# Shared PSUM banks and alternating row halves in the preparation of an RWKV-7 recurrence, inside a two-layer diffusion backbone

## The chip, the cores and the metric

The kernel runs on one core of a Trainium2 chip. The metric is the device time of one execution in microseconds (us). A core has a matrix engine (TensorE, PE in the profile, with its weight loads as PEld), a vector engine (VectorE, DVE), a scalar engine (ScalarE, ACT), a general one (GpSimd, POOL) and a sync engine (SyncE, SP), which here issues the DMAs. Matrix products land in PSUM, which this kernel uses as eight banks of 128 rows by 512 fp32 numbers.

## What is computed

The reference is a flow-matching backbone on 256 context tokens and 512 latent ones (768 together), model width 1024, all fp32. Layer 0 mixes tokens with latent attention (MLA, 8 heads) beside eight RWKV-7 heads of 64; layer 1 with state-space heads beside windowed attention. Each layer ends in a feed-forward part. The change lies in the RWKV-7 part of layer 0, which computes, per head and in both directions,

```python
def rwkv_scan(r, w, k, v, kk, a, state0, reverse):
    def step(s, inp):
        r_t, w_t, k_t, v_t, kk_t, a_t = inp
        sa = jnp.einsum('bhij,bhj->bhi', s, -kk_t)
        s = s * w_t[:, :, None, :] + sa[..., None] * (kk_t * a_t)[:, :, None, :] + v_t[..., None] * k_t[:, :, None, :]
        return s, jnp.einsum('bhij,bhj->bhi', s, r_t)
    ...
    s_final, ys = lax.scan(step, state0, xs, reverse=reverse)
```

The kernel does this in 12 chunks of 64 tokens. Within a chunk the step's dependence on earlier tokens is a triangular system, so each chunk needs the inverse of a 64x64 triangular matrix before the recurrence over chunks can use it.

## The kernel before

The program is written in Python as one long sequence. A scheduler then fixes each engine's order of instructions from that sequence and from its own simulation of the times; each engine runs its instructions in that fixed order and waits at each for its inputs and for a free buffer. Buffers come from named pools: a pool hands out its buffers in turn, and the next user of a buffer waits until the last reader of the one before is done. So both the order and the waits follow from the sequence and from the sizes of the pools. All products that a helper issues carry its line, L267; tiles tell them apart.

PSUM in the stretch concerned: `acc`, two tiles of two banks each, for the projections; `bkp`, one bank, for the layers' modulation (`ada_group`) and small products; `gk`, two banks; `iv`, one bank; and `px1` and `px0`, one bank each for the two halves of the recurrence. `px1` and `px0` are opened when `gk`, `iv`, `bkp` and `accp` are closed in the program, and take over banks of these. After that come `accm` (four banks) and `mb` (two).

The eight heads are four pairs p; the two heads of a pair lie in rows 0 to 63 and 64 to 127 (`par` 0 and 1). For each pair the program does three things:

- `features(p)` (L596): projections, then per direction d the tiles `ar` (two factors of a product, made by three POOL operations of 768 columns at L674, L673, L676), `EC` (small POOL copies at L669 to L672) and `bk` (brought into place by DMA; tile `bkt`). A POOL operation at L649 makes the bonus term.
- `rwkv_prep(p)` (L699): for each direction and each of three groups of four chunks, two sets of four products `bk` by `ar`, one for each row half, 64 rows deep and 128 columns wide, each set in a `gk` bank of its own. ScalarE copies the diagonal blocks out of the bank to `LS` (L721, twice a set) and one to `PB` (L722), VectorE masks the rest (L723, L726), DMAs bring it to the recurrence's records. Then four transposes into another `gk` bank (L732) and a ScalarE copy of it (L733). `LS` has one buffer; POOL's MEMSET at L701 is its first writer.
- `rwkv_inverse(p)` (L738): a VectorE transpose of `LS` to `I`, then 60 POOL operations (L748 a product into a temporary `w`, L750 its sum into `I`, each waiting for the one before), a select (L751) and a MEMSET (L753), which invert the 32x32 diagonal blocks of all the pair's chunks by substitution. VectorE transposes the result to `PN` and `TT` (L755 to L758). Then the joins to 64x64 blocks, for each direction: 24 products `PN` by `PB` into an `iv` bank, a copy to `w1` (L767), 24 products `TT` by `w1` into an `iv` bank, a copy back (L773), a DMA to the records (L775). The temporary `w` and `w1` share two buffers.

The program's order is preparation 0, preparation 1, inverse 0, preparation 2, inverse 1, preparation 3, inverse 2, inverse 3. Then comes `rwkv_chain`, 12 steps times two halves (half 0 has the pairs 0 and 1, half 1 the pairs 2 and 3); each half-step writes two `b` tiles in its `px` bank. Beside it the program writes latent attention: sums of squares, key products (`acc`), value products (`mb`, 36 of them), query products (`acc`), eight heads of attention (`ax` and others), and then the output projection of both mixers.

Of the kernel before, what the change touches and what calls it, by code (L numbers as in the profile page):

```python
# [17 lines left out]
P = 128  # L18
# [192 lines left out]
def hybrid_kernel(ctx: ExitStack, tc: tile.TileContext, a, out):  # L211
# [4 lines left out]
    def open_pool(name, side=None, psum=False):  # L216
        kw = dict(side=side, space=PSUM) if psum else dict(side=side)
        PL[name] = tc.alloc_tile_pool(name=name, bufs=1, reuse_waits="tile", **kw)

    def close_pool(*names):  # L220
        for n in names:
            PL.pop(n).release()

    def T(pool, shape, tag, bufs=1, dt=F32):
        uid[0] += 1
        return PL[pool].tile(shape, dt, tag=tag, bufs=bufs, name=f"{tag}_{uid[0]}")
# [4 lines left out]
    def F(dt=F32):  # L231
        return row_tile("sb", "f", NF, dt)
# [12 lines left out]
    def bank():  # L245
        return T(bankp[0], [P, 512], bankp[1], bankp[2])
# [14 lines left out]
    def mm(o, lhsT, rhs, start, stop, shared=False):  # L261
        i = -1
        if pace["pins"] is not None:
            pace["t"] += o.free_size() / 2400 * (4 if rhs.dtype == F32 else 1) * (0.5 if o.shape[0] == 64 else 1)
            i = min(pace["base"] + int(pace["t"] / pace["per"]), len(pace["pins"]) - 1)
        with tc.issue_after(pace["pins"][i]) if i >= 0 else nullcontext():
            ins = nc.tensor.matmul(o, lhsT=lhsT, rhs=rhs, start=start, stop=stop, skip_group_check=shared)  # L267
        pe_last[0] = ins.ins
# [7 lines left out]
    open_acc("accp", 2)  # L276
    open_bank("bkp", 1)
    open_pool("gk", psum=True)
    open_pool("iv", psum=True)
    con = T("sb", [P, NCO], "con")  # L280
    pv = T("sb", [P, NPV], "pv")
    ones = T("sb", [P, P], "ones")
# [247 lines left out]
    H = (slice(0, 64), slice(64, P))  # L530
# [49 lines left out]
    GC = 4  # L580
# [111 lines left out]
        return ars, bks  # L692

    def gbank():
        return T("gk", [P, 512], "gk", 2)

    Q = [(slice(64 * q, 64 * q + 32), slice(64 * q + 32, 64 * q + 64)) for q in range(2)]

    def rwkv_prep(p, ars, bks):  # L699
        LS = T("pp", [P, 32, 32], "LS", 1)  # L700
        nc.gpsimd.memset(LS[:, :, 24:32], 0.0)  # L701
        PB = T("pp", [P, 2 * NCH, 32], "PB", 2)
        for d in range(2):
            bk, ar = bks[d], ars[d]
            for gi in range(NG):
                i0 = d * NCH + gi * GC
                cg = slice(gi * GC, gi * GC + GC)
                s0 = (gi * GC + 4 * d) % NCH
                rec = REC[p // 2][:, s0:s0 + GC, d, p % 2]
                tg = T("pp", [P, GC, 192], "tg", 2)  # L710
                w = T("pp", [P, GC, 2, CH], "W", 2)
                for par in range(2):
                    hb, hk = H[par], H[1 - par]
                    r0 = Q[par][0]
                    b = gbank().rearrange("p (c x) -> p c x", x=P)
                    for c in range(GC):
                        mm(b[:, c], lhsT=bk[hb, gi * GC + c].rearrange("p a t -> p (a t)"),
                           rhs=ar[hb, gi * GC + c].rearrange("p a t -> p (a t)"), start=True, stop=True)
                    for q in range(2):
                        rr = Q[par][q]  # L720
                        nc.scalar.copy(LS[rr, :, i0:i0 + GC].rearrange("p t i -> p i t"), b[rr, :, 32 * q:32 * q + 32])  # L721
                    nc.scalar.copy(PB[r0, i0:i0 + GC], b[r0, :, 32:64])  # L722
                    tt(out=w[hk], in0=b[hk].rearrange("p c (a t) -> p c a t", a=2),  # L723
                       in1=mk[hk].rearrange("p (a t) -> p a t", a=2).unsqueeze(1).to_broadcast([64, GC, 2, CH]),
                       op=ALU.mult)
                    tt(out=tg[hb, :, 128:192], in0=b[hb, :, 64:128],  # L726
                       in1=mk[hb, 64:].unsqueeze(1).to_broadcast([64, GC, CH]), op=ALU.mult)
                    dma(rec[hk, :, 128 * par:128 * par + 128], w[hk].rearrange("p c a t -> p c (a t)"))

                b = gbank()  # L730
                for c in range(GC):
                    nc.tensor.transpose(b[:, c * P:(c + 1) * P], bk[:, gi * GC + c].rearrange("p a t -> p (a t)"), ident)  # L732
                nc.scalar.copy(tg[:, :, 0:128], b.rearrange("p (c x) -> p c x", x=P))  # L733
                dma(rec[:, :, 256:448], tg)

        return LS, PB

    def rwkv_inverse(p, LS, PB):  # L738

        I = T("pp", [P, 32, 32], "I", 2)  # L740
        TT = T("pp", [P, 32, 64], "TT", 1)
        nc.vector.transpose(I.rearrange("p t s -> p (t s)"), LS.rearrange("p t s -> p (t s)"))
        Jf = T("pp", [P, 384], "w1", 2)
        eng = nc.gpsimd if INV_POOL[p] else nc.vector
        for m in range(1, 31):
            n = 31 - m
            tmp = Jf[:, :n * m].rearrange("p (t s) -> p t s", s=m)
            eng.tensor_tensor(out=tmp, in0=I[:, m + 1:, m:m + 1].to_broadcast([P, n, m]),  # L748
                              in1=I[:, m:m + 1, :m].to_broadcast([P, n, m]), op=ALU.mult)
            eng.tensor_tensor(out=I[:, m + 1:, :m], in0=I[:, m + 1:, :m], in1=tmp, op=ALU.add)  # L750
        nc.gpsimd.affine_select(out=I, in_=I, pattern=[[1, 32], [-1, 32]], compare_op=ALU.is_gt, fill=0.0,  # L751
                                base=0, channel_multiplier=0)
        nc.gpsimd.memset(I.rearrange("p t s -> p (t s)")[:, 0:1024:33], 1.0)  # L753
        PN = T("pp", [P, 32, 32], "PN", 1)
        nc.vector.transpose(PN, I.rearrange("p t s -> p s t"))  # L755
        for r0, r1 in Q:
            nc.vector.transpose(TT[r0, :, :32].rearrange("p i t -> p t i"), I[r0])
            nc.vector.transpose(TT[r1, :, 32:].rearrange("p i t -> p t i"), I[r1])  # L758
            nc.gpsimd.memset(TT[r1, :, :32], 0.0)
        for d in range(2):  # L760
            b = T("iv", [P, 512], "iv", 1)[:, :384].rearrange("p (c x) -> p c x", x=32)
            w1 = T("pp", [P, 384], "w1", 2).rearrange("p (c x) -> p c x", x=32)
            for c in range(NCH):
                for r0, r1 in Q:
                    mm(b[r1, c], lhsT=PB[r0, d * NCH + c], rhs=PN[r0, :, d * NCH + c], start=True, stop=True)
            for r0, r1 in Q:
                nc.scalar.copy(w1[r1], b[r1])  # L767
            b2 = T("iv", [P, 512], "iv", 1)[:, :384].rearrange("p (c x) -> p c x", x=32)
            for c in range(NCH):
                for r0, r1 in Q:  # L770
                    mm(b2[r0, c], lhsT=w1[r1, c], rhs=TT[r1, d * NCH + c, 32:], start=True, stop=True)
            for r0, r1 in Q:
                nc.scalar.copy(TT[r0, d * NCH:d * NCH + NCH, 32:], b2[r0])  # L773
            for cs_, st_ in CMAP[d]:
                dma(REC[p // 2][:, st_, d, p % 2, 448:512], TT[:, d * NCH + cs_.start:d * NCH + cs_.stop])  # L775
# [3 lines left out]
    for p in range(4):  # L779
        fe = features(p)  # L780
        cur = rwkv_prep(p, *fe)
        if pend:
            rwkv_inverse(p - 1, *pend)
        pend = cur
        ada_group(0, p + 2, mods0, "pj", NAW)
    rwkv_inverse(3, *pend)
    close_pool("pp", "pa", "pj", "iv", "gk", "bkp")


    open_pool("rw0", "left")  # L790
# [164 lines left out]
    for tb in range(6):  # L955
        b = bank()
        n = 0
        for k in range(2):
            for (xt, wt) in ((kvh, wvh), (kvl, wvh), (kvh, wvl)):
                mm(b, lhsT=xt[k][:, tb * P:(tb + 1) * P], rhs=wt[:, 4 * k:4 * k + 4].rearrange("p a b -> p (a b)"),  # L960
                   start=n == 0, stop=n == 5)
# [248 lines left out]
    def sdbank():  # L1210
        return T("sd", [P, 512], "sd", 3)
# [77 lines left out]
    for g in range(2):  # L1289
# [7 lines left out]
        t = T("sx", [P, 6, P], "btm", 2)  # L1297
# [11 lines left out]
    for g in range(2):  # L1309
# [10 lines left out]
        for d in range(2):  # L1320
            hprev = None
            hs = slice(32 * d + 8 * g, 32 * d + 8 * g + 8)
            for i, c in enumerate(seq[d][:-1]):
# [4 lines left out]
                b = sdbank()  # L1328
# [9 lines left out]
        b = sdbank()  # L1338
# [8 lines left out]
        for c in range(2, 6):  # L1347
# [20 lines left out]
            b = sdbank()  # L1368
# [41 lines left out]
    t = F()  # L1410
# [136 lines left out]
    for g in range(2):  # L1547
# [12 lines left out]
        b = bank()  # L1560
# [70 lines left out]
```

## Time and profile before

| | |
|---|---|
| median of three timed runs | 2265.78 us (2265.28 to 2267.42) |
| the profiled execution's own time | 2264.21 us |
| its span in the profile | 2262.3 us |
| mean clock granted to TensorE | 0.956 of full speed |
| busy: PE, PEld | 2076.5 us (92%), 1640.9 us (73%) |
| busy: DVE, ACT, POOL | 1346.3 us (60%), 928.3 us (41%), 506.2 us (22%) |

Times in the profile count from the span's start. In a row of the timeline stand the start, the busy time, the engine, the line in the kernel, the operation, what it writes and reads, rows and columns, and the count of instructions that the row sums up; in brackets how long the engine stood idle just before it and what ended that. In a row of the windows view stand the stretch's bounds, its length, then for PE, PEld, DVE, ACT and POOL the busy time with the number of instructions, then the granted clock, the mean busy share of the DMA engines and GB/s. In a row of the grouped view the three numbers are the shortest, the middle and the longest duration in ns, then the first start and the last.

### The profile page before, as it was taken

The numbers are of one execution on the slowest core, as the hardware profiler recorded it, in microseconds if no ns is written. First come the engines' busy times: TensorE is split into PE (matmuls) and PEld (weight loads), VectorE is DVE, ScalarE is ACT, GpSimd is POOL, SyncE is SP. The second block draws the span as 40 slices with busy tenths as digits, with TensorE's granted clock in tenths as the row PEclk, the third lists the DMA queues.
The fourth block names the chain that finished last, engine by engine and source line by source line (L and its number), as shares of the span: only waits on it lengthen the run. The fifth ranks groups of instructions, "written<-read, shape, count | busy, mean of one in ns | idle before, by whom it ended". The sixth has DMA issues, their size and how long they took to land.

```text
span 2262.3 us, 33884 instructions
## 1 busy us (share of the span) xinstructions
PE 2076.5 (92%) x13558; PEld 1640.9 (73%) x13558; DVE 1346.3 (60%) x2081; ACT 928.3 (41%) x1434; POOL 506.2 (22%) x486
## 2 busy tenths in 40 slices
PE   5888889788998999999999998898888999999997
PEld 3666667566654878888888886786565667888886
DVE  5566965666766465445354444678985556554555
ACT  4445663532355244233132335544344345342434
POOL 0027686611223010000000004442641230000000
PEclk9999999698999999999999999999889999999998
DMA  8477777669741441211212213213426032323231
GB/s 303 125 206 206 182 211 195 211 190 320 259 165 42 154 139 62 61 66 57 75 53 60 75 58 114 96 52 117 133 71 172 28 111 79 96 92 98 84 116 61
DMA packets 181069, 282.58 MB, mean 125 GB/s; under 512 B 63328, under 2 KB 118656, under 8 KB 177840
## 3 DMA queue, kind: packets, MB, share of 16 engines
q1 hardware_dynamic: 180912, 280.42, 40.6%
q8 instruction: 107, 1.75, 0.3%
q14 instruction: 50, 0.41, 0.1%
HBM read 225.43 MB, written 47.33 MB: 121 GB/s over the span
## 4 chain that ended last, share of the span: by engine, by line
PE 65%; DVE 6%; ACT 5%; DMA 5%; issue 3%; POOL 1%; SPq 0%; DVEq 0%; ACTq 0%; POOLq 0%
PE acc L267 49%; PE sd L267 3%; PE o L267 3%; PE wo L267 2%; PE ab L267 2%; PE b L267 2%; DMA u<-sp_v 1%; DVE E L1359 1%; DMA aw<-ada 1%; POOL I L750 1%; PE ax L267 1%; PE ad L267 1%; POOL w L748 1%; DMA E<-sp_ac 1%; ACT L416 1%
## 5 line engine op out<-in xcount | busy, mean ns | idle before, releaser
L267 PE MATMUL acc<-s,whi 128*128 128x512 f32 (+1 forms) x3104 | 759.8, 356 | 3.0 <-ACT s L463 3.0
L267 PEld LDWEIGHTS acc<-s,whi 128*128 128x128 f32 x3104 | 546.0, 188 | 97.3 <-ACT s L463 4.8
L267 PE MATMUL acc<-s,wlo 128*128 128x512 f32 (+1 forms) x1552 | 462.0, 358 | 0.0
L267 PE MATMUL acc<-h,whi 128*128 128x256 f32 (+2 forms) x1248 | 321.1, 371 | 15.9 <-ACT p L639 5.0
L325 ACT CAST whi<-wraw 128x1024 fp32r<-128x1024 f32 (+5 forms) x228 | 210.0, 923 | 282.3 <-PE acc L267 218.0
L267 PEld LDWEIGHTS acc<-s,wlo 128*128 128x128 f32 x1552 | 289.5, 188 | 42.9 <-DVE wlo L326 0.7
L267 PEld LDWEIGHTS acc<-h,whi 128*128 128x128 f32 (+1 forms) x1248 | 223.7, 197 | 68.4 <-issue 15.4
L326 DVE TENSOR_TENSOR wlo<-wraw,whi 128x1024 fp32r<-128x1024 f32 (+5 forms) x205 | 218.7, 1069 | 44.2 <-ACT whi L325 43.6
L381 DVE SCALAR_TENSOR_TENSOR s<-acc,pv,s 128x511 f32<-128x511 f32 (+1 forms) x132 | 87.0, 659 | 246.2 <-ACT s L380 245.4
L380 ACT ACTIVATE s<-acc,pv 128x512 f32<-128x512 f32 (+1 forms) x132 | 93.4, 708 | 235.4 <-PE acc L267 224.2
L484 DVE SCALAR_TENSOR_TENSOR x<-acc,mods,x 128x512 f32<-128x512 f32 (+1 forms) x136 | 79.4, 620 | 175.0 <-PE acc L267 174.8
L267 PE MATMUL acc<-h,wlo 128*128 128x256 f32 (+2 forms) x624 | 179.5, 362 | 0.0
L434 POOL TENSOR_TENSOR f<-f,f 128x768 f32<-128x768 f32 (+1 forms) x24 | 31.3, 1306 | 635.0 <-ACT f L429 625.1
L267 PEld LDWEIGHTS acc<-h,wlo 128*128 128x128 f32 (+1 forms) x624 | 119.3, 195 | 21.9 <-issue 5.6
L1178 POOL TENSOR_TENSOR s<-w,s 128x256 f32<-128x256 f32 x6 | 5.0, 855 | 381.3 <-ACT s L416 381.3
L383 DVE SCALAR_TENSOR_TENSOR s<-acc,pv,s 128x511 f32<-128x511 f32 (+1 forms) x132 | 87.2, 660 | 4.2
L750 POOL TENSOR_TENSOR I<-I,w 128x30 f32<-128x30 f32 (+14 forms) x120 | 76.7, 639 | 9.0
L748 POOL TENSOR_TENSOR w<-I 128x30 f32<-128x30 f32 (+14 forms) x120 | 69.4, 578 | 34.6 <-PE iv L267 25.8
L387 ACT CAST s<-s 128x768 fp32r<-128x768 f32 (+1 forms) x44 | 32.0, 727 | 106.1 <-DVE s L1151 106.1
L326 POOL TENSOR_TENSOR wlo<-wraw,whi 128x1024 fp32r<-128x1024 f32 x23 | 61.7, 2686 | 59.6 <-ACT whi L325 56.1
L1359 DVE TENSOR_SCALAR E<-E,acm 128x128 f32<-128x128 f32 x128 | 61.2, 546 | 14.6 <-ACT G L1356 14.6
L723 DVE TENSOR_TENSOR W<-gk,con 64x512 f32<-64x512 f32 x48 | 32.8, 683 | 51.2 <-ACT PB L722 47.3
(390 smaller groups left out, 3347.3 us busy)
## 6 DMA issues: line engine op xcount, KB each, us to landing
aw<-ada SPq DMA_DIRECT2D x96, 512.0 KB, 5.8
wraw<-up SPq DMA_DIRECT2D x88, 512.0 KB, 3.5
rec<-sp_rec SPq DMA_DIRECT2D x24, 1024.0 KB, 9.7
wraw<-w_in SPq DMA_DIRECT2D x47, 512.0 KB, 3.8
wraw<-down SPq DMA_DIRECT2D x40, 384.0 KB, 3.1
sp_rec<-tg SPq DMA_DIRECT2D x24, 384.0 KB, 3.3
E<-sp_ac SPq DMA_DIRECT2D x16, 512.0 KB, 5.5
x<-xT SPq DMA_DIRECT2D x16, 384.0 KB, 5.9
```

Source lines behind the costliest of these rows:

```text
L267: ins = nc.tensor.matmul(o, lhsT=lhsT, rhs=rhs, start=start, stop=stop, skip_group_check=shared)
L325: nc.scalar.copy(hi[:, :kt], raw[:, :kt])
L326: (eng or tt)(out=lo[:, :kt], in0=raw[:, :kt], in1=hi[:, :kt].bitcast(F32), op=ALU.subtract)
L380: act(o[rows, t0:t0 + n], ps[rows, po:po + n], AF.Identity, scale=w1, bias=b)
L381: stt(out=o[rows, t0 + 1:t0 + n], in0=ps[rows, po:po + n - 1], scalar=w0, in1=o[rows, t0 + 1:t0 + n], op0=ALU.mult, op1=ALU.add)
L383: stt(out=o[rows, t0:t0 + n - 1], in0=ps[rows, po + 1:po + n], scalar=w2, in1=o[rows, t0:t0 + n - 1], op0=ALU.mult, op1=ALU.add)
L387: nc.scalar.copy(hi, src)
L484: stt(out=x[:, t0:t0 + n], in0=ps[:, po:po + n], scalar=mods[:, c6 * 8 + m, c:c + 1], in1=x[:, t0:t0 + n], op0=ALU.mult, op1=ALU.add)
L723: tt(out=w[hk], in0=b[hk].rearrange("p c (a t) -> p c a t", a=2), in1=mk[hk].rearrange("p (a t) -> p a t", a=2).unsqueeze(1).to_broadcast( ...
L748: eng.tensor_tensor(out=tmp, in0=I[:, m + 1:, m:m + 1].to_broadcast([P, n, m]), in1=I[:, m:m + 1, :m].to_broadcast([P, n, m]), op=ALU.mult)
L750: eng.tensor_tensor(out=I[:, m + 1:, :m], in0=I[:, m + 1:, :m], in1=tmp, op=ALU.add)
L1359: ts(out=e[:, h], in0=e[:, h], scalar1=acm[:, c, h0 + h:h0 + h + 1], scalar2=0.0, op0=ALU.subtract, op1=ALU.min)
```

## The change

The pool `iv` is gone, and `gk` has three banks in place of two. The products, the transposes and the joins of the inverse all take their bank from `gk` in turn. In a preparation's group, both product banks are taken first, and the eight products are written alternately for the two row halves; what follows each half is unchanged.

```diff
     open_pool("gk", psum=True)
-    open_pool("iv", psum=True)
...
     def gbank():
-        return T("gk", [P, 512], "gk", 2)
+        return T("gk", [P, 512], "gk", 3)
...
+                gb = [gbank().rearrange("p (c x) -> p c x", x=P) for _ in range(2)]
+                for c in range(GC):
+                    for par in range(2):
+                        mm(gb[par][:, c], lhsT=bk[H[par], gi * GC + c].rearrange("p a t -> p (a t)"),
+                           rhs=ar[H[par], gi * GC + c].rearrange("p a t -> p (a t)"), start=True, stop=True)
                 for par in range(2):
                     hb, hk = H[par], H[1 - par]
                     r0 = Q[par][0]
-                    b = gbank().rearrange("p (c x) -> p c x", x=P)
-                    for c in range(GC):
-                        mm(b[:, c], lhsT=bk[hb, gi * GC + c].rearrange("p a t -> p (a t)"),
-                           rhs=ar[hb, gi * GC + c].rearrange("p a t -> p (a t)"), start=True, stop=True)
+                    b = gb[par]
...
         for d in range(2):
-            b = T("iv", [P, 512], "iv", 1)[:, :384].rearrange("p (c x) -> p c x", x=32)
+            b = gbank()[:, :384].rearrange("p (c x) -> p c x", x=32)
...
-            b2 = T("iv", [P, 512], "iv", 1)[:, :384].rearrange("p (c x) -> p c x", x=32)
+            b2 = gbank()[:, :384].rearrange("p (c x) -> p c x", x=32)
...
-    close_pool("pp", "pa", "pj", "iv", "gk", "bkp")
+    close_pool("pp", "pa", "pj", "gk", "bkp")
```

The scheduler answers with another order on every engine between the first product of preparation 0 and the output projection. In the rows below, the line numbers of the changed kernel are one or two off those of the kernel before, and the numbers behind the tiles' names tell buffers apart; they differ between the kernels for the same tile.

The first place is TensorE in the first group of preparation 3: `gk` is written by the products (`ar`, `bkt`) of the two row halves and by the transposes (`con`). Before, in the same group:

```order
L267 MATMUL acc_3771<-h_295,wlo_3657 128x512
L267 MATMUL gk_3030<-ar_2916,bkt_2917 128x128 x4
L267 MATMUL gk_3041<-ar_2916,bkt_2917 128x128 x4
L267 MATMUL acc_3771<-h_327,whi_3656 128x256
L267 MATMUL acc_3771<-h_327,whi_3656 128x512
```

Now:

```order
L267 MATMUL gk_3027<-ar_2913,bkt_2914 128x128
L267 MATMUL gk_3028<-ar_2913,bkt_2914 128x128
L267 MATMUL gk_3027<-ar_2913,bkt_2914 128x128
L267 MATMUL gk_3028<-ar_2913,bkt_2914 128x128
L267 MATMUL gk_3027<-ar_2913,bkt_2914 128x128
L267 MATMUL gk_3028<-ar_2913,bkt_2914 128x128
L267 MATMUL gk_3027<-ar_2913,bkt_2914 128x128
L267 MATMUL gk_3028<-ar_2913,bkt_2914 128x128
L734 MATMUL gk_3049<-con_67,bkt_2914 128x128 x4
```

The four products of the second half stood behind the four of the first; now the halves alternate one by one, each into its own bank. Not every group follows the program here: the scheduler still puts some groups' halves one behind the other.

The second place is POOL at the end of inverse 1. `w` and `I` are the inverse; `ar`, `EC` and `f` are features of pair 3. Before:

```order
L748 TENSOR_TENSOR w_355_2405<-I_2402 128x108
L674 TENSOR_TENSOR ar_2916<-p_2918,p_2871 128x12x64
L750 TENSOR_TENSOR I_2402<-I_2402,w_355_2405 128x4x27
L669 COPY EC_95_569<-ar_2916 128x12
L748 TENSOR_TENSOR w_355_2405<-I_2402 128x84
L673 TENSOR_TENSOR ar_2916<-f_2698,ar_2916 128x12x64
L750 TENSOR_TENSOR I_2402<-I_2402,w_355_2405 128x3x28
L649 TENSOR_SCALAR f_2822<-f_2822,pv_71 128x768
L748 TENSOR_TENSOR w_355_2405<-I_2402 128x58
L676 TENSOR_TENSOR ar_2916<-p_2899,ar_2916 128x12x64
```

Now, from the last operations of inverse 1 (`I_2399`) to the first of inverse 2 (`I_3149`):

```order
L752 TENSOR_TENSOR I_2399<-I_2399,w_355_2402 128x2x29
L700 MEMSET LS_2960 128x32x8
L750 TENSOR_TENSOR w_355_2402<-I_2399 128x30
L752 TENSOR_TENSOR I_2399<-I_2399,w_355_2402 128x30
L753 AFFINE_SELECT I_2399<-I_2399 128x1024
L755 MEMSET I_2399 128x32
L750 TENSOR_TENSOR w_450_3152<-I_3149 128x30
L752 TENSOR_TENSOR I_3149<-I_3149,w_450_3152 128x30
L750 TENSOR_TENSOR w_450_3152<-I_3149 128x58
L673 TENSOR_TENSOR ar_2913<-p_2915,p_2868 128x12x64
L752 TENSOR_TENSOR I_3149<-I_3149,w_450_3152 128x29x2
L673 TENSOR_TENSOR ar_2935<-p_2937,p_2882 128x12x64
```

Pair 3's feature operations moved from among the last operations of inverse 1 to among the first of inverse 2, and the MEMSET of `LS` for pair 3 now stands ahead of the last operations of inverse 1.

The third place is TensorE around the joins and the start of the recurrence, whose products are `b` (half 0 here). Before, from the first join product of inverse 2 on:

```order
L267 MATMUL iv_3226<-PN_3218,PB_2215 32x32 x24
L267 MATMUL b_3934<-u_3911,rec_3910 64x64 x8
L267 MATMUL iv_3254<-TT_3153,w_453_3227 32x32
L267 MATMUL b_3934<-rs_3943,rec_3910 64x64 x8
L267 MATMUL iv_3254<-TT_3153,w_453_3227 32x32 x23
```

Now, from the first join product of inverse 3 on:

```order
L267 MATMUL gk_3464<-PN_3456,PB_2962 32x32 x24
L267 MATMUL gk_3492<-TT_3391,w_473_3465 32x32
L267 MATMUL gk_3520<-PN_3456,PB_2962 32x32 x24
L267 MATMUL acc_5616<-u_5454,whi_5573 128x256
L267 MATMUL acc_5616<-u_5454,whi_5573 128x512
L267 MATMUL gk_3548<-TT_3391,w_476_3521 32x32
L267 MATMUL gk_3492<-TT_3391,w_473_3465 32x32 x23
L267 MATMUL gk_3548<-TT_3391,w_476_3521 32x32 x23
```

And 22 rows of key and query products (`acc`) further on, the first `b` with the first of the value products (`mb`):

```order
L267 MATMUL acc_5616<-u_5464,whi_5573 128x256
L267 MATMUL acc_5616<-u_5464,whi_5573 128x512
L267 MATMUL b_3930<-u_3907,rec_3906 64x64 x8
L267 MATMUL mb_5474<-whi_3770,u_5444 128x512
L267 MATMUL mb_5474<-whi_3770,u_5445 128x512
```

The recurrence's first product moved from behind inverse 2's first join product to behind inverse 3's last one, and all value products moved behind that point with it.

## The prediction

> **What bounds the kernel now.** I read the page first. The whole chain that ended last is TensorE by two thirds, so the question is where TensorE runs dry.
>
> ```profile
> span 2262.3 us, 33884 instructions
> PE 65%; DVE 6%; ACT 5%; DMA 5%; issue 3%; POOL 1%; SPq 0%; DVEq 0%; ACTq 0%; POOLq 0%
> ```
>
> Then I compared the two kernels' instruction orders. They agree up to the first product of the recurrence's preparation and again from the output projection on, whose first rows in the timeline are these (start, busy time, engine, operation, tiles, count):
>
> ```profile
> 141.50 1.71 PE L267 MATMUL gk<-ar,bkt 64*128 64x128 f32 x16
> 746.14 0.62 PE L267 MATMUL acc<-u,whi 128*128 128x256 f32 x2 [1.51 <-ACT u L387]
> ```
>
> So only these 605 us can change, and I read them in four stretches of the windows view (PE busy, granted clock as PEclk, then DMA share).
>
> ```profile
> 403.00:486.00 83.00, 64.01 (x796) 50.87 (x796) 56.31 (x64) 36.86 (x65) 42.77 (x66) 0.77 0.57 176
> 486.00:504.00 18.00, 17.92 (x198) 14.83 (x193) 12.59 (x22) 6.29 (x16) 0.00 (x0) 1.00 0.97 278
> 504.00:526.00 22.00, 15.57 (x306) 13.30 (x302) 15.91 (x36) 7.65 (x16) 0.00 (x0) 0.77 1.03 360
> 526.00:746.00 220.00, 201.38 (x2157) 128.94 (x2156) 150.42 (x270) 91.16 (x152) 60.90 (x47) 0.97 0.60 189
> ```
>
> TensorE stands idle for 19.0 us between the end of the preparation (403) and the end of inverse 3 (486), for 6.4 us until attention starts (526), and for 18.6 us of the 220 after that. It never has much slack: what it may do, and when, decides.
>
> What it waits for is POOL. Each head pair's inverse is 60 POOL operations in a row, and the next inverse begins only after the one before has had its first join product (both use the two `w1` buffers). In brackets stands the idle time before an operation.
>
> ```profile
> 266.65 0.56 POOL L748 TENSOR_TENSOR w<-I 128x30 f32<-128x30 f32 x1
> 312.35 0.37 POOL L748 TENSOR_TENSOR w<-I 128x108 f32<-128x108 f32 x1
> 316.94 1.81 POOL L674 TENSOR_TENSOR ar<-p,p 128x768 f32<-128x768 f32 x1 [4.21 <-DMA sp_v<-p]
> 338.50 0.18 POOL L753 MEMSET I<- 128x32 f32 x1
> 353.47 0.80 POOL L748 TENSOR_TENSOR w<-I 128x30 f32<-128x30 f32 x1 [12.41 <-PE iv L267]
> 402.58 0.16 POOL L753 MEMSET I<- 128x32 f32 x1
> 416.11 0.25 POOL L748 TENSOR_TENSOR w<-I 128x30 f32<-128x30 f32 x1 [13.37 <-PE iv L267]
> 463.73 0.16 POOL L753 MEMSET I<- 128x32 f32 x1
> ```
>
> Inverses 1, 2, 3 end at 338.7, 402.7 and 463.9. A clear inverse takes 47.8 us (416.11 to 463.89), the step to the next 14.8 and 13.4 us. Inverse 1 was held up: at 312.35 only 8 operations were left, and feature operations of pair 3 stood among them.
>
> TensorE's side of the same stretch, in order of time: first step of the recurrence, the three joins of inverse 3, the last query product, the first of attention.
>
> ```profile
> 409.80 0.45 PE L267 MATMUL b<-u,rec 128*64 128x64 f32 x2 [1.36 <-DMA u<-sp_v]
> 465.98 1.53 PE L267 MATMUL iv<-PN,PB 32*32 32x32 f32 x48 [1.18 <-DVE PN L755]
> 473.54 1.48 PE L267 MATMUL iv<-TT,w 32*32 32x32 f32 x46 [3.47 <-DVE TT L758]
> 485.39 0.95 PE L267 MATMUL iv<-TT,w 32*32 32x32 f32 x48
> 503.21 0.61 PE L267 MATMUL acc<-u,whi 128*128 128x256 f32 x2
> 526.13 0.73 PE L267 MATMUL ax<-kh,qh 128*128 128x512 f32 x2
> ```
>
> The recurrence of half 0 needs only inverses 0 and 1, and starts at 409.80, 76 us before inverse 3 is joined. That early start is why TensorE idles only 19 us there.
>
> **The change part by part.** (1) Alternating halves. Of the 24 pairs of four products, 15 stand next to each other today (one row of 16) and 9 apart (two rows of 8). In the new order 10 alternate, 10 are next to each other, 4 apart.
>
> ```profile
> 149.75 1.16 PE L267 MATMUL gk<-ar,bkt 64*128 64x128 f32 x8
> L721 ACT COPY LS<-gk x96: 362/376/418, 142.7 to 402.2; 32x128 f32<-32x128 f32 x96
> L722 ACT COPY PB<-gk x48: 255/257/260, 143.5 to 402.6; 32x128 f32<-32x128 f32 x48
> L733 ACT COPY tg<-gk x24: 567/586/592, 148.3 to 403.4; 128x512 f32<-128x512 f32 x24
> ```
>
> No row shows an alternating pair. At worst it takes what neighbours take, the 1.71 us at 141.50; at best one half hides in the other, 1.16 us. Two halves back to back take 0.61 us less than two alone (2.32), so they do overlap where they meet; I take 1.2. Before: 15 x 1.71 + 9 x 2.32 = 46.5 us. After: 10 x 1.71 + 4 x 2.32 + 10 x 1.2 = 38.4. That saves TensorE 8 us (3 to 8.5), but in front of POOL's chain, so it moves the end only if POOL's chain moves.
>
> The copies out of the bank are not changed: per group ScalarE has 4 x 0.376 + 2 x 0.257 + 0.586 = 2.6 us, more than TensorE's 1.71. The Trainium skill, page "TensorEngine Tiling (Array Packing)", section "Performance Considerations", speaks against the change here: tiling speeds up TensorE but not PSUM evacuation, so the copies may become the bottleneck. By that rule the 8 us would be worth nothing; by full use of the row they would be 8; the sum below holds 0 for them either way.
>
> (2) POOL's order. As its rows in the section on the change show, pair 3's feature operations (`ar`, `EC`, `f`) stood between the last operations of inverse 1; now they stand between the first of inverse 2. Inverse 1 loses the features and gains a wait: the MEMSET of `LS` must see preparation 2 copied out. The features move into inverse 2:
>
> ```profile
> L674 POOL TENSOR_TENSOR ar<-p,p x8: 1801/2190/3283, 109.1 to 330.6; 128x768 f32<-128x768 f32 x8
> L673 POOL TENSOR_TENSOR ar<-f,ar x8: 1811/2502/3356, 116.5 to 338.6; 128x768 f32<-128x768 f32 x8
> L676 POOL TENSOR_TENSOR ar<-p,ar x8: 1828/2334/2575, 120.8 to 336.7; 128x768 f32<-128x768 f32 x8
> 323.49 2.21 POOL L649 TENSOR_SCALAR f<-f,pv 128x768 f32<-128x768 f32 x1
> ```
>
> That is 2 x (2.19 + 2.50 + 2.33) + 2.21 = 16.3 us. Inverse 1 ends at about 318 (312.7, 7 short operations, the select), if the wait for `LS` adds nothing; + 14.8 = 333; inverse 2 takes 47.8 + 16.3 = 64 and ends at 397 (402.7 before); + 13.4 + 47.8: inverse 3 ends at 458, its first product stands at 460 instead of 466. The two directions' joins now follow each other in three banks, so the last comes about 10 us later (9.0 from 465.98 to 475.02 today), at 470 instead of 486.
>
> (3) The recurrence's first step. Its result banks px0 and px1 take the room of the closed pools. So far px0's was free once preparation 3 was done; now all inverses run through the three shared banks. In TensorE's rows (section on the change) the first `b` of half 0 moved from behind inverse 2's first product to behind inverse 3's last one and 22 key and query products, and all 36 value products `mb` with it. Behind the wait for inverse 3 TensorE's queue now holds 152 key and query products, 36 `mb` and the first 7 banks of `b`:
>
> ```profile
> 483.91 0.85 PE L267 MATMUL acc<-u,whi 128*128 128x256 f32 x4
> 484.61 0.51 PE L267 MATMUL acc<-u,wlo 128*128 128x256 f32 x2
> 484.95 0.51 PE L267 MATMUL acc<-u,whi 128*128 128x256 f32 x2
> 445.44 0.73 PE L267 MATMUL mb<-whi,u 128*128 128x512 f32 x2
> 448.08 0.39 PE L267 MATMUL mb<-wlo,u 128*128 128x512 f32 x1
> 486.27 0.68 PE L267 MATMUL b<-rs,rec 64*64 64x64 f32 x16
> 492.73 0.69 PE L267 MATMUL b<-u,rec 128*64 128x64 f32 x16
> 497.36 1.30 PE L267 MATMUL b<-rec,u 128*64 128x64 f32 x32
> ```
>
> Six `acc` take 1.04 us (483.91 to the next at 484.95, the sum of their starts), 0.173 each: 26.3 us. Twelve `mb` from 445.44 to 448.08 take 0.24 each: 8.6. The banks: 7 x 0.69 + 4 x 0.68 + 3 x 1.30 = 11.4. From 470 this ends at 516, where the last query product stands at 503.8 today: 12.5 us late. TensorE's new idle time lies in front: of the 64.01 + 17.92 = 81.9 us that it works from 403 to 504 today, 46.3 now stand behind the join and 36 ahead of it, 28 with the 8 saved.
>
> **The sum.** After the last query product TensorE spends 22 us today, 15.57 of them on nine `b` banks, while the DMA share is 1.03. In the new order four banks stand there: 4 x 0.69 + 2 x 0.68 + 2 x 1.30 = 6.7. With the casts of the first head it may be 8 to 22 us; I take 10, nearest to the work itself: attention starts at 526, as now. But the recurrence is then six banks further back, 6 x (0.69 + about 1.0) = 10 us, in a stretch that has 18.6 us idle in 220; I let 1 us vanish. So +9: 2273 against the profiled 2264.2 (span 2262.3), which lies 1.6 under the median of 2265.8. Forecast 2275.
>
> A second count agrees: from 397 to 470 TensorE idles 73 - 28 = 45 us where it idles 19 today, 26 more; less the 8 saved and the 6 by which POOL's part of the stage starts earlier, the last query product comes 12 late.
>
> A longer wait has a second price. The Trainium skill, page "TensorE: Matmul & The Clock Gate", section "Why this matters for your kernels", says that an idle gap over about 3 us drops the clock to half until it has been busy some 4 us. The trace agrees as far as it goes: 0.77 was granted in the two stretches with idle time above, 1.00 between them. By it the wait would cost some 2 us more (an estimate from that page); the sum goes without.
>
> **The rivals.** (A) Faster: POOL's chain comes much earlier. If preparations 1 and 2 finish sooner with three banks, inverse 1 could start at 255 instead of 266.65 and nothing holds its `LS`. Then inverse 3's first product stands at 447 to 450, attention starts 11 us earlier, and half of the lag is absorbed: 2265.8 - 11 + 4 = 2259 (2255 if all of it is). It decides from 450 on downwards. For it speaks the third bank; against it, that pair 2's features are ready only at about 255 and share POOL with inverse 1.
>
> (B) No change: the idle 18.6 us after 526 take up the recurrence's lag entirely, since late attention waits on its own chain; 2265.8 - 1 = 2265.
>
> (C) Slower still: the gap before attention stays at 22 us because DMA is full, +12 on the forecast: 2287. For it speaks the DMA share of 1.03.
>
> (D) Alternation does nothing, since the copies bound it: the preparation ends 8 us later than I have it. POOL's chain hides that unless the MEMSET of `LS` waits for it; then it is 2283 at most. This is what the page on array packing named above would make of it.
>
> **How the numbers follow.** What a measurement of this kernel can tell from no change is about 0.2%, 4.5 us. Forecast 0.36, C 0.10, D 0.08: slower 0.54. B and the near edges: same 0.18. A: faster 0.28. The likeliest case alone is 2269 to 2281. The range takes in A with all of the lag absorbed and C with the 2 us of a slower clock: 2254 to 2289.
>
> **What would show it.** Right: the first `b` of TensorE after inverse 3's last join, near 472; idle time of 40 us or more between inverse 2 and that join; pair 3's `ar` inside inverse 2; alternating products of 16 records in about 1.2 us. Wrong: inverse 3's first product before 450, an attention start before 518, or an output projection that starts no later than 746.

## The result and the profile after

The changed kernel takes 2302.27 us (median of four runs, 2297.25 to 2306.1) against 2266.45 us (2265.28 to 2267.42); the ratio is 1.0151, 95% interval 1.0137 to 1.0166. It is slower, as forecast, by about 36 us where 9 were forecast, and lies above the range. The profiled execution took 2297.25 us with a span of 2295.4, against 2262.3 before, so 33.1 us of span are to be found.

Up to the start of attention the steps came near the times that were written down. POOL's rows of the changed kernel, start and end of its inverses 1, 2 and 3:

```profile
247.46 3.53 POOL L750 TENSOR_TENSOR w<-I 128x30 f32<-128x30 f32 x1 [10.68 <-PE gk L267]
318.34 0.16 POOL L755 MEMSET I<- 128x32 f32 x1
331.16 1.50 POOL L750 TENSOR_TENSOR w<-I 128x30 f32<-128x30 f32 x1 [12.66 <-PE gk L267]
392.88 0.16 POOL L755 MEMSET I<- 128x32 f32 x1
405.63 0.25 POOL L750 TENSOR_TENSOR w<-I 128x30 f32<-128x30 f32 x1 [11.90 <-DVE W L725]
451.51 0.16 POOL L755 MEMSET I<- 128x32 f32 x1
```

TensorE's rows of the same kernel: the second group of products, now alternating; first and last join of inverse 3; the first `b`; the end of the query products; attention; the recurrence's last finish product; the output projection.

```profile
148.45 1.16 PE L267 MATMUL gk<-ar,bkt 64*128 64x128 f32 x16
453.67 1.56 PE L267 MATMUL gk<-PN,PB 32*32 32x32 f32 x48 [2.77 <-DVE PN L757]
461.38 2.76 PE L267 MATMUL gk<-TT,w 32*32 32x32 f32 x92 [1.12 <-DVE TT L760]
470.66 0.69 PE L267 MATMUL b<-u,rec 128*64 128x64 f32 x16
512.60 0.51 PE L267 MATMUL acc<-u,whi 128*128 128x256 f32 x2
523.04 1.22 PE L267 MATMUL ax<-kh,qh 128*128 128x512 f32 x2 [1.98 <-ACT qh L386]
773.52 1.65 PE L267 MATMUL b<-sg,g 128*128 128x384 f32 x2 [3.66 <-DVE rf L907]
776.69 1.01 PE L267 MATMUL acc<-u,whi 128*128 128x256 f32 x2 [1.52 <-ACT u L386]
```

Attention starts 3 us earlier than before (523.04 against 526.13), and yet the last stretch of the output projection starts at 776.69 instead of 746.14. So 30.6 of the 33.1 us are lost by 776.69, all of them after attention has started. The windows view of the changed kernel:

```profile
397.00:470.60 73.60, 35.71 (x411) 26.99 (x410) 36.62 (x31) 30.12 (x46) 41.80 (x66) 0.58 0.41 114
470.60:523.00 52.40, 47.59 (x551) 40.01 (x550) 33.43 (x63) 19.81 (x44) 0.00 (x0) 0.95 0.87 285
523.00:776.70 253.70, 218.66 (x2431) 142.34 (x2431) 160.69 (x299) 98.81 (x163) 59.80 (x47) 0.93 0.57 186
700.00:776.70 76.70, 55.38 (x272) 31.59 (x270) 44.49 (x65) 45.44 (x59) 16.73 (x14) 0.89 0.31 112
```

From attention's start on TensorE has 218.66 us of work where it had 201.38, which is 17.3 more, and idles 35.0 us where it idled 18.6, 16.4 more. Less the 3 us earlier start, that is the 30.6. Most of the idle time sits at the very end: 21.3 us of it in the last 76.7.

What happens there is shown by ScalarE. At the end of the recurrence each pair is finished (`rwkv_finish`): mean, variance, normalisation, bonus, gate. It squares the pair's centred result once (`Y<-rf`), so these rows count the pairs; `rs<-b` is the copy in the recurrence's last step. Before:

```profile
636.91 0.84 ACT L893 ACTIVATE Y<-rf 128x768 f32<-128x768 f32 x1
668.85 0.84 ACT L893 ACTIVATE Y<-rf 128x768 f32<-128x768 f32 x1 [2.07 <-DVE rf L892]
686.12 0.37 ACT L821 COPY rs<-b 128x256 f32<-128x256 f32 x1 [1.75 <-PE b L267]
706.50 0.85 ACT L893 ACTIVATE Y<-rf 128x768 f32<-128x768 f32 x1 [0.82 <-DVE rf L892]
731.28 0.84 ACT L893 ACTIVATE Y<-rf 128x768 f32<-128x768 f32 x1 [0.24 <-DVE rf L892]
```

And after:

```profile
687.05 0.37 ACT L823 COPY rs<-b 128x256 f32<-128x256 f32 x1
696.77 0.85 ACT L895 ACTIVATE Y<-rf 128x768 f32<-128x768 f32 x1 [2.70 <-DVE rf L894]
722.86 0.84 ACT L895 ACTIVATE Y<-rf 128x768 f32<-128x768 f32 x1 [0.81 <-DVE rf L894]
741.94 0.84 ACT L895 ACTIVATE Y<-rf 128x768 f32<-128x768 f32 x1 [2.82 <-DVE rf L894]
763.48 0.84 ACT L895 ACTIVATE Y<-rf 128x768 f32<-128x768 f32 x1 [2.20 <-DVE rf L894]
```

The last step of the recurrence is at 687.05 in the changed kernel; before it is at 686.12, so the recurrence as a whole ends on time. But before, half 0 had run four steps ahead, and its two pairs were finished (636.91, 668.85) while half 1 was still at its steps. Now the halves go in turn, both end at 687, and all four pairs queue up behind, 22 us apart (66.7 over three intervals). The spacing is that of one pair after the other: the three buffers `rf` hold one pair's `yc`, `rn` and bonus.

That gave the theory for the runs, called theory 1: half 0's lost head start costs the time, because its finish falls into the tail. Its rivals: the alternating products themselves (rival 2), or TensorE's idle time and the late value products before the join (rival 3).

### The profile page after: what moved, and what is told of

Its sections match the earlier page's. It is cut to its first block, busy times and chain, and to the rows that moved or that the text cites. A ratio compares the mean times of both kernels' runs of the same rounds, so it can differ in the third digit from the quotient of the medians.

```text
span 2295.4 us, 33864 instructions
## 1 busy us (share of the span) xinstructions
PE 2077.7 (91%) x13558; PEld 1637.7 (71%) x13558; DVE 1349.5 (59%) x2081; ACT 932.0 (41%) x1436; POOL 509.6 (22%) x486
## 4 chain that ended last, share of the span: by engine, by line
PE 70%; DVE 9%; DMA 7%; ACT 6%; issue 3%; POOL 2%; SPq 1%; DVEq 0%; ACTq 0%; POOLq 0%
PE acc L267 52%; PE b L267 3%; PE sd L267 3%; PE o L267 3%; PE ab L267 2%; DMA aw<-ada 2%; PE wo L267 2%; PE gk L267 2%; DVE E L1361 1%; PE ax L267 1%; DMA E<-sp_ac 1%; POOL w L750 1%; POOL I L752 1%; DVE x L461 1%; PE ad L267 1%
## 5 line engine op out<-in xcount | busy, mean ns | idle before, releaser
L267 PE MATMUL acc<-s,wlo 128*128 128x512 f32 (+1 forms) x1552 | 456.3, 354 | 0.0
L750 POOL TENSOR_TENSOR w<-I 128x30 f32<-128x30 f32 (+14 forms) x120 | 75.2, 626 | 43.8 <-PE gk L267 23.3
L1236 DVE SCALAR_TENSOR_TENSOR f<-acc,pv,f 128x510 f32<-128x510 f32 (+3 forms) x80 | 48.5, 612 | 22.9 <-ACT f L1232 21.4
```

The costliest lines, as they stand in the source:

```text
L1236: stt(out=o[:, t0 + lo:t0 + hi], in0=ps[:, po + lo + s:po + hi + s], scalar=col(f"sconv_w{tap}", j), in1=o[:, t0 + lo:t0 + hi], op0=ALU.mu ...
```

## The experiments

Each ratio below is to the kernel before, run again beside the version in question (medians 2267 to 2268 us), with its 95% interval. "The loss" is the 36 us of the changed kernel.

**The shared banks alone.** Edit against the changed kernel: each half's four products follow its own `gbank()` again.

> Only the shared banks: iv is gone and gk has three banks, but each half's four products are written one set behind the other as in the kernel before. In TensorE's order the first b still stands behind inverse 3's last join, and the halves of the recurrence go in turn (0A 0B 1A 1B, A being half 0). Theory 1 (the loss is half 0's lost head start of four steps, since its finish then falls into the tail): 2295 to 2306, as the changed kernel. Rival 2 (the alternation itself costs): 2262 to 2270. Rival 3 (TensorE's idle time before the late join, value products included): 2295 to 2306 too.

Measured 2306.12 us, ratio 1.0155 (1.0130 to 1.0179): the whole loss is there without the alternation. Rival 2 falls as its cause. What three shared banks do to the products `bk` by `ar` can be read here too: they take 47.6 us, where they took 51.9 before and take 43.1 in the changed kernel.

```profile
L267 PE MATMUL gk<-ar,bkt 64*128 64x128 f32 x384 | 47.6, 304 | 8.2 <-ACT tg L732 4.9 <-issue 2.3 <-DVE tg L725 0.9
```

**The alternation alone.** Edit against the kernel before: only the loop over `c` and `par` of the diff; pools as before.

> Only the alternation: gk has two banks and iv one, as before; both banks of a group are taken first and the halves alternate. Half 0 has its head start (0A 1A 2A 3A 0B). Theory 1: as before, 2258 to 2267, and TensorE is busy 5 to 9 us less with the products of ar and bkt (43 to 47 us in place of 51.9). Rival 2 (alternation costs): 2290 or more. Rival 3: 2258 to 2267.

Measured 2289.74 us, ratio 1.0093 (1.0076 to 1.0110). Theory 1 missed this one clearly: the head start is there, the recurrence's last finish product is at 747 (before 744), and still 22 us are lost. Its products of `ar` and `bkt` take 51.2 us against 51.9: with two banks they save next to nothing, but they don't cost anything either. On TensorE they hardly alternate: one row of 16 takes 1.17 us, all others 1.65 us or more. What is late is attention, whose first product starts at 539.65 and whose last comes 27 us later than before. The view of waits, 536 to 541:

```profile
DVE ql L388 <- ACT qh L387: 5.8, 1, 5.8
ACT qh L387 <- DMA f<-sp_q: 5.6, 2, 5.4
PEld ax L267 <- ACT qh L387: 5.2, 1, 5.2
PE ax L267 <- ACT qh L387: 5.1, 1, 5.1
```

TensorE waits for ScalarE's cast of the first query head, and that for the head's load `f<-sp_q`. The rows of SP's DMA queue before, where these loads and the records (`rec`, 1 MB each) stand in one line:

```profile
504.75 0.34 SPq L805 DMA_DIRECT2D rec<-sp_rec  x1
...
515.34 0.33 SPq L983 DMA_DIRECT2D sp_q<-f  x1
516.01 0.32 SPq L1002 DMA_DIRECT2D f<-sp_q  x1
```

And in this run:

```profile
521.55 0.35 SPq L986 DMA_DIRECT2D sp_q<-f  x1
521.94 0.43 SPq L1005 DMA_DIRECT2D f<-sp_k  x1
522.79 0.59 SPq L808 DMA_DIRECT2D rec<-sp_rec  x1
523.49 1.49 SPq L810 DMA_DIRECT2D u<-sp_v  x2
525.07 0.59 SPq L808 DMA_DIRECT2D rec<-sp_rec  x1
525.76 1.75 SPq L810 DMA_DIRECT2D u<-sp_v  x2
527.59 0.55 SPq L1005 DMA_DIRECT2D f<-sp_q  x1
```

Two more loads of records now stand ahead of the query's load, which is issued at 527.59 instead of 516.01. That this order of the queue is a second cause was called theory Q. It would account for the late start, 13.5 of the 27 us by which attention ends late; why attention also takes longer is not shown. In the changed kernel, whose attention starts at 523, it is not at work.

**The changed kernel with half 0's bank free.** Only the order in which PSUM pools are opened differs, so that px0 lies on `bkp`'s bank:

```diff
-    open_bank("bkp", 1)
     open_pool("gk", psum=True)
+    open_bank("bkp", 1)
...
-    open_pool("px1", "right", psum=True)
     open_pool("px0", "right", psum=True)
+    open_pool("px1", "right", psum=True)
```

> The changed kernel, with one difference: half 0's result bank px0 takes over the bank of bkp, which no join uses, in place of one of the three shared ones (pool gk is opened ahead of bkp, px0 ahead of px1). In TensorE's order half 0 is five steps ahead again; the value products still stand behind inverse 3's last join. Theory 1 (head start): the loss is gone, 2255 to 2272, half 0's last step before 630 and the output projection at 735 to 750. Rival 3 (idle time before the join and the late value products): 2285 to 2300, since those stay. Rival 2 (alternation): 2290 or more.

Measured 2269.58 us, ratio 1.0003 (0.9990 to 1.0016): the loss is gone. The first `b` is at 393.66, the last finish product at 725. Its value products are nearly as late as in the changed kernel (first at 463; there at 471, before at 433), so rival 3 falls.

**The kernel before with half 0's bank late.** The same swap of px0 and px1 alone, in the kernel before, which puts px0 on `iv`'s bank.

> The kernel before, with one difference: px0 is opened ahead of px1, so that half 0's result bank is the one of iv, which is free only after inverse 3's last join. Banks, joins, products and the value products (early, during inverse 2's and 3's wait) stay as before; the halves go in turn. Theory 1 (head start): 2285 to 2302. Rival 3 (late joins and late value products): 2264 to 2272, since none of these is later. Rival 2 (alternation): 2266.

Measured 2291.22 us, ratio 1.0103 (1.0081 to 1.0124): two swapped lines (and the order of closing that goes with them) bring two thirds of the loss into a kernel whose program is otherwise untouched. Its value products are early (first at 436), and it doesn't help. The first `b` is at 493. The recurrence's last step comes 9 us earlier than before (677.46 against 686.12), and yet its last finish product is 25 us later, at 769 (the second of the two in the last row):

```profile
493.38 0.69 PE L267 MATMUL b<-u,rec 128*64 128x64 f32 x16
677.46 0.37 ACT L821 COPY rs<-b 128x256 f32<-128x256 f32 x1
768.35 1.65 PE L267 MATMUL b<-sg,g 128*128 128x384 f32 x2 [3.22 <-DVE rf L905]
```

**The free bank without the alternation.** The edits of the first and third run together.

> As e3 (three shared banks, px0 in bkp's bank), without the alternation. Half 0 is five steps ahead of half 1 at first, as in e3. Theory 1 (time follows the later of two ends, the recurrence's finish and attention's last head; the alternation itself is worth little): 2262 to 2275, within 0.4% of e3. A theory in which the alternation costs by itself (as the run of the alternation alone, plus 0.93%, could be read): 15 us or more below e3, so 2255 or less.

Measured 2278.27 us, ratio 1.0047 (1.0034 to 1.0060). This is 0.44% above the third run, some 10 us, and 3 us above what theory 1 gave. Nothing here says that the alternation costs. But attention starts at 539 here and at 525 in the third run, so the 10 us are no clean price of its absence either.

**The joins of inverses 2 and 3 apart.** Pools in the order of the third run, px1 ahead of px0, and `(gbank() if p < 2 else bank())` for the joins.

> As the changed kernel, but the joins of inverses 2 and 3 go through bkp's one bank, as they did through iv's; gk (three banks, the alternation kept) is opened ahead of bkp, so px0 takes a gk bank that is free after preparation 3 and px1 takes bkp's. The value products stand ahead of inverse 3's joins again. The scheduler lets half 0 run only two steps ahead (0A 1A 0B 2A 1B 3A). Theory 1 (head start): between the two: half of the loss, 2275 to 2292, with the recurrence's last finish product between 750 and 768. Rival 3 (idle time before the join, late value products): 2260 to 2272, as both are gone.

Measured 2278.86 us, ratio 1.0053 (1.0031 to 1.0075), with the last finish product at 755: with a head start of two steps about a third of the loss is left, inside what theory 1 gave. Rival 3 misses again: the value products are early here (first at 428), and the time is not that of the kernel before.

**The alternation in pairs 0 to 2, and in pair 3.** The edit of the second run, under `if p < 3` and `if p == 3`.

> The kernel before with the alternation alone, in pairs 0, 1 and 2 only. The order of the DMA queue around the start of attention is that of the kernel before: ten loads of recurrence records ahead of attention's first query load. Theory Q (the run of the alternation alone was slow because two more loads of records, 1 MB each, were queued ahead of that load): as before, 2258 to 2270. Rival (alternating products cost by themselves): three quarters of 22 us, 2280 to 2287.

> The kernel before with the alternation alone, in pair 3 only. Twelve loads of records stand ahead of attention's first query load, as where all pairs alternate. Theory Q (queue order): the whole loss, 2282 to 2292, and attention starts at 536 or later. Rival (alternating products cost by themselves): one quarter of 22 us, 2268 to 2274.

Measured 2267.86 us, ratio 1.0005 (0.9992 to 1.0018), and 2288.70 us, ratio 1.0085 (1.0062 to 1.0109). The edit in three pairs costs nothing, in the fourth it costs everything, so it is the order that the scheduler makes of it, not the products. That the place of the query's load is what matters in that order fits both runs (it is issued at 522.60 and 527.69), but no run moved this load alone. Attention starts at 532 in the first and at 540.46 in the second, after a wait for the same cast:

```profile
540.46 1.22 PE L267 MATMUL ax<-kh,qh 128*128 128x512 f32 x2 [6.50 <-ACT qh L387]
```

**The finish side by side.** Edit in the changed kernel:

```diff
-        yc = row_tile("rwb", "rf", 3)
-        rn = row_tile("rwb", "rf", 3)
+        if p % 2 == 0:
+            rec2[p // 2] = [rec_rows(p // 2, dt) for dt in (F32, F32, F32R)]
+        yc, rn = rec2[p // 2][p % 2]
...
-        for p in range(4):
+        for p in (0, 2, 1, 3):
```

> The changed kernel; only rwkv_finish differs: pairs of different halves may be finished side by side (order 0, 2, 1, 3; yc and rn of a half in its own free rec buffers, so that the three rf buffers hold only the bonus), where the three rf buffers let the pairs pass only one after the other. The halves still go in turn, both ending near 687. Theory 1 in its sharper form (the loss is that all four finishes fall behind the last step, one after the other, 22 us each): the finish after 687 takes 45 to 60 us in place of 88, the time falls to 2272 to 2290. Rival (the finish's order doesn't matter; TensorE's work and idle time set the end): 2295 to 2306.

Measured 2271.41 us, ratio 1.0021 (1.0007 to 1.0034), some 30 us under the changed kernel, though the first `b` is still at 470.56 and the halves go in turn. The squares of the four pairs are now 14 us apart instead of 22:

```profile
687.36 0.85 ACT L896 ACTIVATE Y<-rec 128x768 f32<-128x768 f32 x1
701.14 0.84 ACT L896 ACTIVATE Y<-rec 128x768 f32<-128x768 f32 x1
715.22 0.85 ACT L896 ACTIVATE Y<-rec 128x768 f32<-128x768 f32 x1 [0.31 <-DVE rec L895]
728.94 0.84 ACT L896 ACTIVATE Y<-rec 128x768 f32<-128x768 f32 x1
```

The whole finish takes 66 us after the last step (682.0 to 748) instead of 88. That is less of a saving than expected (45 to 60 us), and yet the time falls to just under the range given. So what the late bank costs is mainly the pile of finishes, not the late start as such. Now attention's last product, at 751, is the later end.

**Both causes avoided.** Pools as in the run with the late joins apart, but only inverse 3's joins in `bkp`'s bank (`p < 3`); once with two `rec` buffers, once with three.

> A version meant to have the change's gain without its loss: three shared banks and alternation, but inverse 3's joins go through bkp's bank; gk is opened ahead of bkp, so that px0 and the value products' banks are free before inverse 3's joins; and two rec buffers in place of three, so that half 0 can't load far ahead (ten loads of records ahead of attention's first query load, as in the kernel before). Theory 1 with theory Q (both causes gone, TensorE's 8 us saved): 2250 to 2264. Rival (the 8 us lie beside POOL's chain and are worth nothing): 2264 to 2270.

> As e11 with three rec buffers: half 0 is five steps ahead and twelve loads of records stand ahead of attention's first query load. Theory Q: 8 to 20 us above e11, with attention starting 5 us or more later than there. Rival (the number of loads in the queue doesn't matter): within 4 us of e11.

Measured 2263.63 us, ratio 0.9981 (0.9968 to 0.9993), and 2256.15 us, ratio 0.9953 (0.9938 to 0.9968). The first lies on the border between its two expectations and decides nothing. The second is faster than both kernels, by 10.8 us than the kernel before and by some 46 us than the changed one. Here theory Q missed as it was put, and so did its rival: with twelve loads ahead attention starts at 520.35, earlier than with ten (522.72), and the time is 7.5 us below, not above or level. So the number of loads isn't the measure. The query's load is issued at 512.92 here, with no load of records between it and the key's load ahead of it; in the run of the alternation alone two stood there. Half 0 begins at 408 in both of these runs and at 412 in that one, so its early start is hardly the reason, and what makes the order so stays open.

```profile
506.92 0.37 SPq L807 DMA_DIRECT2D rec<-sp_rec  x1
509.87 0.33 SPq L985 DMA_DIRECT2D sp_q<-f  x1
...
512.45 0.42 SPq L1004 DMA_DIRECT2D f<-sp_k  x1
512.92 1.28 SPq L1004 DMA_DIRECT2D f<-sp_q  x1
```

**The best version without the alternation.**

> As e12 (three shared banks, inverse 3's joins in bkp's bank, px0 free early), without the alternation. Half 0 is four steps ahead; 14 loads of records stand ahead of attention's first query load (12 in e12). If the alternation is worth the TensorE time that it saves in the products of ar and bkt (6 us: 41 against 47 to 48 us) where nothing else hides it: 2260 to 2266. If it lies beside POOL's chain: within 3 us of e12, 2253 to 2259.

Measured 2270.65 us, ratio 1.0014 (1.0002 to 1.0026): 0.6% or 14 us above the version with it, more than either side gave, while the products of `ar` and `bkt` take 45.2 us against 41.1. The last finish product is at 727, but attention starts at 535 and ends at 742 (520 and 728 with the alternation). The query's load is issued at 524.83 instead of 512.92. So again the difference goes with attention's place in the queue, and what the alternation is worth by itself stays open beyond the 4 us of TensorE's time.

One table holds all profiled executions, some of which lie a few us above their kernel's median. It has the start of the last finish product, the start of attention's last product `o`, and the execution's own time, each in us.

| kernel | last finish | last `o` | time |
|---|---|---|---|
| before | 744 | 734 | 2264 |
| changed | 774 | 748 | 2297 |
| shared banks alone | 784 | 753 | 2309 |
| alternation alone | 747 | 761 | 2290 |
| changed, px0 free | 725 | 740 | 2264 |
| before, px0 late | 769 | 741 | 2297 |
| px0 free, no alternation | 755 | 756 | 2286 |
| joins of 2 and 3 apart | 755 | 740 | 2283 |
| alternation, pairs 0 to 2 | 753 | 743 | 2275 |
| alternation, pair 3 | 754 | 768 | 2295 |
| finish side by side | 748 | 751 | 2276 |
| last join apart, two `rec` | 727 | 738 | 2263 |
| last join apart | 730 | 728 | 2256 |
| the same, no alternation | 727 | 742 | 2268 |

In each row the time is the later of the two ends plus 1520 to 1530 us. The output projection needs both, and what follows it takes the same within these 10 us. An edit in the preparation is worth what it does to the later of them. In all fourteen executions attention starts 7 to 13 us after its query's first load is issued, but from there to its last `o` it takes anything from 207 to 228 us. So the load's issue goes with attention's start, and does not by itself set its end.

## Why the prediction was right in its sign and wrong in its size

The alternating halves: forecast 1.2 us a group and 8 us in all, a sum that also held five groups whose halves came next to each other. Measured 1.16, and 51.9 against 43.1 us in the grouped view, so 8.8 us. About half of it is not the alternation's: the shared banks alone bring 51.9 to 47.6, the alternation 47.6 to 43.1. (The forecast's own sums, 46.5 and 38.4, priced every row like the shortest; the difference came out all the same.) The row of the changed kernel:

```profile
L267 PE MATMUL gk<-ar,bkt 64*128 64x128 f32 x384 | 43.1, 305 | 7.5 <-ACT tg L735 3.8 <-issue 2.5 <-DVE tg L728 0.9
```

TensorE's idle time in front of these products is 7.5 us, 3.8 of it until ScalarE's copy `tg` is done; before it was 4.0 and 1.1. The Trainium skill, page "TensorEngine Tiling (Array Packing)", section "Performance Considerations", warns that evacuation does not speed up with the products. No run here shows that it held the faster products back: with the shared banks alone, where the halves don't alternate, the idle time is 8.2 us and 4.9. That the saving moves no end, as the sum had it, holds for the changed kernel.

POOL's order and the late join: right, and a little early. Inverse 1 ended at 318.5 (318), inverse 3 at 451.7 (458), its joins at 464 (470). But the 318 was luck. Inverse 1 started 19 us earlier than before (247.46 against 266.65), which the forecast did not count on and rival A did; and the wait for `LS`, which the forecast put at nothing, held it for 9 us, until VectorE's transpose at the head of inverse 2 had read the `LS` before:

```profile
306.85 0.30 POOL L752 TENSOR_TENSOR I<-I,w 128x58 f32<-128x58 f32 x1
316.10 0.32 POOL L700 MEMSET LS<- 128x256 f32 x1 [8.95 <-DVE I L744]
```

Without that wait inverse 1 would have ended near 309.5 (an estimate, 318.5 less 8.95). The first `b` came at 470.66 (near 472), the last query product at 513 (516), attention at 523 (526). From 397 to 470.6 TensorE idled 37.9 us (45 forecast).

The step that failed is this one: "the recurrence is then six banks further back, 6 x (0.69 + about 1.0) = 10 us, in a stretch that has 18.6 us idle in 220; I let 1 us vanish. So +9". It counts the lag in TensorE's work, carries it to the end of the stage and expects the idle time to take some of it. The lag itself was about right: from attention's start on TensorE has 272 more records of `b` than before (1552 against 1280: 96 more of `b<-u,rec`, 48 of `b<-rs,rec`, 128 of `b<-rec,u`), which at the prices of the prediction's rows are 11.4 us. The rest of the 17.3 us is, on balance, the same products taking longer, at a granted clock of 0.93 instead of 0.97. What failed is the path from the lag to the end. By the last step the lag was gone (687.05 against 686.12), as rival B had it, and yet the time was lost: the idle time did not shrink by 1 us but grew by 16.4. The sum has no term for what follows the last step, the finish of four pairs with six `b` banks each, which runs pair by pair through ScalarE and VectorE at 22 us a pair. Before, half 0's two finishes lay under half 1's steps. The head start was read as a filler of idle time, where its use was the stagger at the end. So the forecast had the origin of the loss right, half 0's late first step. Its sign came true by another path than the lag that it counted, and in that it was lucky.

None of the rivals had this mechanism. Rival C ended 2287 by another way, a gap in front of attention from a full DMA queue. That gap did not appear in the changed kernel (10.4 us from 512.60 to 523.04, forecast 10). Rival A's 447 to 450 for inverse 3's first product was missed by 4 us (453.67): the early start that it named came, but `LS` was waited for. Coming near it bought nothing, since attention's start is not the end that counts. Rival D's premise, that the alternation saves nothing, did not hold (47.6 to 43.1 us).

The clock: the granted clock was 0.58 from 397 to 470.6 and 0.89 in the last 76.7 us, against 0.77 and 0.94 to 0.97 in the stretches of before. The page "TensorE: Matmul & The Clock Gate" of the Trainium skill, section "Why this matters for your kernels", which sets the clock back after idle gaps, would have it so, and the trace agrees. The first products of the output projection's last stretch still pay for it: at 776.69 two take 1.01 us, at 746.14 before 0.62, with a granted clock of 0.50 from 770 to 780 against 1.00 from 740 to 750 before.

## What to carry to other kernels

When a change delays one of two parallel chains, follow each to what consumes it, through its epilogue (the work behind its last step), and ask whether the epilogues overlapped because the chains were staggered; the last step's time alone says nothing. When a bank or buffer pool is merged, look who inherits its memory afterwards: here the order in which two pools were opened was worth 23 us. Where a scheduler orders the queues, a local edit can move a load behind megabytes of others, so compare the place of the first load of each stage before pricing the edit itself.

## What the runs showed that was not expected

Alternating products of two row halves, each into its own bank, overlap almost fully: 16 records take 1.16 us, as long as 8 of one half alone (1.16). With two banks in the pool the same program order saved almost nothing (51.2 against 51.9 us), because the scheduler left hardly any of it; with three banks it saved 4.5 (47.6 to 43.1), and the third bank by itself 4.3.

One load's place in a DMA queue goes with a loss nearly as large as the late bank's: in the run of the alternation alone the query's first load was issued 11.6 us later (527.59 against 516.01), attention started 13.5 us later, and the execution took 22 us more. That the load's place alone does it is not shown.
